# Group C's low-rank inputs projected with features as rows, their squares summed at reload, and four-head query jobs in a new order

## The chip, the cores and the metric

The kernel runs on one core of one Trainium2 chip. The time is the device time of one execution in microseconds, as the median of several runs. TensorE (PE) multiplies matrices and transposes, VectorE (DVE) and ScalarE (ACT) work elementwise, GpSimd (POOL) does a few products, and SyncE (SP) issues nearly all transfers between HBM and the on-chip memory. Matmul results go to PSUM, which has eight banks.

## The reference, cut to what matters

Two layers of a mixer. In each, one input projection feeds three groups of attention heads and a gate. 512 latent tokens and 256 context tokens go through the same weights; in the second layer context tokens need keys and values only.

```python
h = rms(x, norm_w[l]) * (1.0 + scale[:, None]) + shift[:, None]
u = h @ w_in
qa, ka, va, qb, kb, vb, cq, ckv, kpe, z = jnp.split(u, split_points(), axis=-1)
qa = rms(heads(qa, H_A), qn_a)                                  # group A, 8 heads of 64
qb = rms(heads(qb, H_B), qn_b)                                  # group B, 12 heads, 4 key/value heads
qc = rms(heads(rms(cq, qa_norm) @ w_qb, H_C), qn_c)             # cq: 768 low-rank features
kvc = heads(rms(ckv, kva_norm) @ w_kvb, H_C)                    # ckv: 512 low-rank features
...
x = x + gate[:, None] * merge_out(o_a, o_b, o_c, z, w_out[l])
```

Group C's queries, keys and values come from a second projection of cq and ckv. Their rms norms need, per token, the sum of squares over all 768 or 512 features. The norm's factor is a number per token, so it can be applied behind the second projection.

## The kernel before, in words

**Numbers as pairs.** Every float32 operand is split into a high and a low part, and each product is made of three matmuls: high x high, high x low, low x high. Weight pieces of 128x512 are loaded (`ws`), split by ScalarE (`wh`) and VectorE (`wl`), and used. The normalised input h lies on the chip as 16 pairs of tiles, 128 features x 768 tokens each; these 32 tiles come from the pool `s3`, which has 52 tiles in all. Heads' queries (one tile per head), keys (two), values (one), tables and probabilities come from the same pool.

**Two kinds of projection jobs.** `TJob` (line 429) puts tokens in rows: the stationary operand is a 128x128 block of h, the weights stream, 256 columns in most jobs; the results of two token tiles fill a PSUM bank. A job has eight steps of two k-blocks each. `FJob` (line 524) puts features in rows: a 128x128 weight block is stationary, and h streams, 384 tokens wide in two halves in layer 0 or 512 wide in layer 1; a job has four steps of four k-blocks and yields 128 features for all tokens. The gate z is made with FJobs (`zjob`, line 1487), and so is the shared rotary key (`kpe`, with the weights stacked).

**Chunks.** `kv_job` and `q_job` (lines 1529 and 1532) are TJobs of four 64-wide blocks. A key/value job has two key heads and two value heads. A query job has two heads of group A and two blocks of low-rank features (kind `"c"`), or three heads of group B and one such block; cq's 12 blocks ride along this way, and ckv's eight fill two jobs of four blocks (`GC`, "C"). Behind each job `post_chunk` (line 936) copies the banks out, squares them on ScalarE, sums the squares per block on VectorE, turns these into norms (`rsqrt`), applies the rotary tables for group B, transposes every pair of blocks on TensorE, and writes the heads' tiles. For blocks of kind `"c"` the sums go into `ssc`, and the transposed block is stored to HBM (`cscr`).

**Reload.** `prep_C` and `prep_one` (lines 1585 and 1608) load the low-rank features back, 128 at a time, four tiles of ckv and then six of cq, and split them into pairs with the gain applied. It takes three tiles of `s3` for each, and only when seven are free. `prep_norm` (line 1594) makes the norms `rq_eps` and `rkv` from `ssc`. `free_h` (line 926) gives the 32 tiles of h back when the last gate job is done. Then `q_jobs(0)` (line 1624) begins the second projection, followed by `w_kvb` jobs and group C's attention.

**What sets the order.** The kernel is recorded by a planner written in Python (`Weaver`, line 77). Strands of work run against an estimated clock of each engine, and each instruction is put on its engine's queue when the planner's turn comes; on the chip every queue runs in this order and waits on semaphores. The main strand runs the list of jobs one after the other; two worker strands run attention units in between, other strands load weights, split them and compute the modulation of the next layer (`ada_vec`, on VectorE). Where the free tiles do not suffice, a strand stands still: a job's last step waits until `room` (line 1109) finds tiles for its results plus two.

**The list of jobs** (layer 0; `layer`, line 1321, at its end): group A in four turns of one key/value job, one gate job, one query job of two heads, then attention of these two heads. The first turn's key/value and query jobs are cut in halves, with three gate jobs between. Group B in four turns: a key/value job in every other one, one or two gate jobs, a query job of three heads, attention. Then the two jobs of ckv, kpe, and the last gate jobs. Layer 1 has the same list with another first turn, and its query jobs cover four token tiles.

Of the kernel before, what the change touches and what calls it, by code (L numbers as in the profile page):

```python
# [18 lines left out]
OP = mybir.AluOpType  # L19
# [504 lines left out]
class FJob:  # L524


    def __init__(self, K, W, c0, segs, rhs, evs, post, stack=False, room=None):
        self.K, self.W, self.c0, self.segs = K, W, c0, segs
        self.rhs, self.evs, self.post, self.stack, self.room = rhs, evs, post, stack, room
        self.ps = [None] * len(segs)  # L530
        self.np = 4
        self.inS = False
        self.done = [Event() for _ in segs]
# [12 lines left out]
    def step(self, p):  # L546
# [32 lines left out]
        K.drop(hi, lo)  # L579

# [34 lines left out]
def body(K):  # L615
# [41 lines left out]
    ssc = K.st([128, 6, 20], name="ssc")  # L657
# [268 lines left out]
    def free_h():  # L926
        for k in range(KT):
            K.put("s3", hT[0][k], hT[1][k])
            hT[0][k] = hT[1][k] = None
        return None  # L930
# [5 lines left out]
    def post_chunk(G, grp, blocks, tiles, cscr, ev_c, rope, part=None):  # L936
# [9 lines left out]
        def gen(ps, done):  # L946
# [5 lines left out]
            for b, ts in enumerate(banks):  # L952
# [31 lines left out]
                if nn < ns:  # L984
                    c0 = blocks[nn][1]
                    nc.vector.tensor_copy(ssc[:, ts[0]:ts[0] + 2, c0:c0 + ns - nn],
                                          ss[:, b * 2 * ns:(b + 1) * 2 * ns].rearrange("p (t b) -> p t b", b=ns)[:, :, nn:])
                    w.bump("dve", 0.1)
# [26 lines left out]
            for bp in range(ns // 2):  # L1015
                pair = blocks[2 * bp:2 * bp + 2]
                pk = [b[0] for b in pair]
                for seg in ("lat", "ctx"):
# [6 lines left out]
                    for b in bs:  # L1025
                        for ti in range(len(banks[b])):
                            o = pt[:, i * 128:(i + 1) * 128]
                            if grp == "A" and seg == "lat" and pk[0] != "c":
                                o = pt.rearrange("p (b r c) -> p r b c", b=4 if pk[0] == "q" else 8, r=8)[:, 2 * i:2 * i + 2]
                            K.tr(o, raws[b][:, ti * 256 + bp * 128:ti * 256 + bp * 128 + 128])  # L1030
                            i += 1
# [3 lines left out]
                    if pk[0] != "c" and (rope is None or seg == "ctx"):  # L1035
                        j = (0 if grp == "A" else 2) + (pk[0] == "k")
                        gain = colA[:, j:j + 1]
                    if "c" in pk:
                        a = pk.index("c") * 64
                        st = yield from K.get("tm")  # L1040
                        yield from K.act(st[a:, :n], pt[a:, :n])
                        keep = w.cur.ft
                        i = blocks[2 * bp + a // 64][1]
                        yield from K.store(cscr[i * 64:i * 64 + 128 - a, c0:c0 + n], st[a:, :n], (128 - a) * n * 4)
                        for x in pk[a // 64:]:
                            K.set(ev_c[i, seg])
                            i += 1
                        K.put("tm", st)
                        w.cur.ft = keep
                    for j, (kind, hd) in enumerate(pair):  # L1050
                        if kind == "c":
                            continue
# [68 lines left out]
    def room_chunk(G, blocks):  # L1121
        d = []
        for kind, i in blocks:
            d += {"q": [(G.Q, i)], "k": [(G.KH, i), (G.KL, i)], "v": [(G.V, i)], "c": []}[kind]
# [196 lines left out]
    def layer(l):  # L1321
# [17 lines left out]
        def small():  # L1339
# [3 lines left out]
            for j in range(4):  # L1343
                K.side(rowB[:, j * 64:(j + 1) * 64], bc(t["qn_b" if j < 3 else "kn_b"][l], 64))
# [11 lines left out]
            yield from K.ts(rowB[:, :192], rowB[:, :192], 0.125, OP.mult)  # L1356
# [149 lines left out]
        def chunk(G, grp, blocks, tiles, cut=None):  # L1506

            runs = []
            for kind, i in blocks:
                c0 = COL["cq"] + 64 * i if kind == "c" else COL[START[kind][grp == "B"]] + 64 * i  # L1510
# [7 lines left out]
            def post(ps, done):  # L1518
# [4 lines left out]
                yield from post_chunk(G, grp, blocks, tiles, cscr, ev_c, rope, part)(ps, done)  # L1523
# [8 lines left out]
        def q_job(G, grp, heads, c, cut=None):  # L1532
            return chunk(G, grp, [("q", h) for h in heads] + [("c", i) for i in c], qt, cut)
# [3 lines left out]
        ev_c = {(i, s): Event() for i in range(20) for s in ("lat", "ctx") if s == "lat" or i >= 12 or not last}  # L1537
# [47 lines left out]
        def prep_C():  # L1585
            for key, nf, n, gain, b0 in (("kv", 4, TOK, kvaT, 12), ("q", 6, ntok, qaT, 0)):
                for f in range(nf):
# [3 lines left out]
                    w.spawn(prep_one(key, f, n, gain, b0 + 2 * f, raw, hi, lo), 2)  # L1591
                    yield None

        def prep_norm():
            yield from K.wait(*ev_c.values())
            tot = yield from sm()
            nt = len(qt)
            yield from K.red(tot[:, 0:nt], ssc[:, 0:nt, 0:12])
            yield from K.ts(tot[:, 0:nt], tot[:, 0:nt], 1.0 / 768, OP.mult, EPS, OP.add)
            yield from K.ts(rq_eps[:, 0:nt], tot[:, 0:nt], EPS, OP.mult)  # L1600
            yield from K.red(tot[:, 8:14], ssc[:, :, 12:20])
            yield from K.rsqrt(rkv, tot[:, 8:14], 1.0 / 512)
            K.put("sm", tot)
            K.set(ev_rkv)

        ev_rkv = Event()

        def prep_one(key, f, n, gain, b, raw, hi, lo):
            yield from K.wait(*(e for (i, _), e in ev_c.items() if i in (b, b + 1)))
            yield from K.load(raw[:, :n], cscr[b * 64:b * 64 + 128, :n], 512 * n)  # L1610
            yield from K.hilo(hi[:, :n], lo[:, :n], raw[:, :n], gain[:, f:f + 1])
            K.put("s3", raw)
            cT[key, f] = (hi, lo)
            K.set(ev_cT[key, f])
            K.put("ck", 0)

# [12 lines left out]
        def post_qC(p, rnd):  # L1629
            def gen(ps, done):  # L1630
                yield from K.wait(ev_kpe, ev_rkv)
# [316 lines left out]
        for p in range(4):  # L1948
            cut = HALF if not last and p == 0 else None
            kv = kv_job(GA, "A", 2 * p, cut)  # L1950
            q = q_job(GA, "A", (2 * p, 2 * p + 1), (2 * p, 2 * p + 1), cut)
            if cut:

                zs = [zjob(f) for f in (10, 11, 12)]
                q[0].inS = zs[2].inS = True
                jobs.extend([Group([kv[0], q[0]]), Group(zs), Group([kv[1], q[1]]), zjob(p)])
            elif last:
                z = zjob(p)
                jobs.extend([kv, z, q] if p else [Group([q, z]), kv])
            else:  # L1960
                jobs.extend([kv, zjob(p), q])
            J(lambda p=p: [attend64(GA, "A", h, h, h // 2) for h in (2 * p, 2 * p + 1)] and None)
            if p == 2:
                J(lambda: w.spawn(prep_B(), 1))
        zq = {0: [4, 5], 1: [6], 2: [7, 8], 3: [9]}
        for g in range(4):
            if g % 2 == 0:
                jobs.append(kv_job(GB, "B", g))
            for f in zq[g]:
                jobs.append(zjob(f))  # L1970
            jobs.append(q_job(GB, "B", range(3 * g, 3 * g + 3), (8 + g,)))
            J(lambda g=g: [attend64(GB, "B", h, g, 4 + h // 2) for h in range(3 * g, 3 * g + 3)] and None)
        for i in (12, 16):
            jobs.append(chunk(GC, "C", [("c", i + j) for j in range(4)], allt))
        jobs.append(FJob(K, W, COL["kpe"], [(0, 384), (384, 768)], rhs_h, ev_h, post_kpe, stack=True))
        J(lambda: (w.spawn(prep_C(), 3), w.spawn(prep_norm(), 2)) and None)
        for f in range(10 if last else 13, KT):
            jobs.append(zjob(f))
        J(free_h)
# [167 lines left out]
```

## Time and profile before

| what | value |
|---|---|
| median of 3 runs | 2937.42 us (2935.22 to 2939.45) |
| the profiled execution, whole | 2933.86 us |
| its span, first to last instruction | 2932.0 us |
| instructions | 54116 |
| busy: PE, PEld | 2808.8 us, 2645.5 us |
| busy: DVE, ACT, POOL | 2013.5 us, 1237.3 us, 148.5 us |
| mean granted TensorE clock | 0.989 of full speed |

PE is the matmuls, PEld the loads of the stationary operand, which overlap them. A row of the groups reads: line, engine, operation, output and inputs by tile name, shapes, count, then busy time and mean nanoseconds of one, then idle time of the engine ahead of it and what ended that. Nearly every matmul has line 333 and every transpose line 336, since helpers record them, so groups are told apart by tiles and shapes: `g<-wh,s` is a matmul of a TJob, `g<-s,wh` one of an FJob, `S<-s,s` are scores, `g<-pt,s` probabilities times values. A row of the timeline starts with the start time and the duration; a duration holds the pipeline's length, so the pace is read from start to start.

### The profile page before, as it was taken

What the parts mean: (1) busy time and instruction counts of PE and PEld (TensorE: products, weight loads), DVE (VectorE), ACT (ScalarE), POOL (GpSimd) and SP (SyncE); (2) the same over time, 40 slices, a digit from 0 to 9 for tenths busy, and PEclk for the clock granted to TensorE, in tenths of its full rate; (3) what the DMA queues carried; (4) which work ended last, traced back from release to release, by engine and by line L of the source; (5) the groups of instructions that cost most, each with busy time, mean ns of one, the idle gap of its engine ahead of it and who ended that gap; (6) DMA issues with size and microseconds to landing.
All of it is one profiled execution on the core that took longest, in us unless ns stands there. A gap on an engine that the chain in (4) does not pass through costs nothing.

```text
span 2932.0 us, 54116 instructions
## 1 busy us (share of the span) xinstructions
PE 2808.8 (96%) x20218; PEld 2645.5 (90%) x20218; DVE 2013.5 (69%) x5277; ACT 1237.3 (42%) x2692; POOL 148.5 (5%) x221
## 2 busy tenths in 40 slices
PE   5999999999999999989999999999999999999998
PEld 3779999999999999979998789999998999889987
DVE  6247776676887878989964385666667686488643
ACT  5223443342543554546421263434444455356421
POOL 3000100000111001000000000000000000000000
PEclk9999999999999999999999999999999999999999
DMA  9764433433323234323443453444342423412253
GB/s 263 248 193 122 115 107 112 116 95 111 90 81 98 85 109 148 121 75 128 144 135 118 126 156 103 116 116 117 92 116 67 114 84 103 137 45 85 90 176 118
DMA packets 408119, 350.09 MB, mean 119 GB/s; under 512 B 66532, under 2 KB 336914, under 8 KB 407856
## 3 DMA queue, kind: packets, MB, share of 16 engines
q1 hardware_dynamic: 405984, 345.32, 39.6%
q8 instruction: 159, 2.61, 0.4%
q0 software_dynamic: 1872, 1.32, 0.4%
q14 instruction: 104, 0.85, 0.1%
HBM read 305.01 MB, written 32.07 MB: 115 GB/s over the span
## 4 chain that ended last, share of the span: by engine, by line
PE 79%; DVE 11%; DMA 5%; SPq 2%; issue 2%; ACT 2%; DVEq 0%; ACTq 0%
PE g L333 63%; PE S L333 9%; PE g L336 5%; DMA s<-w_ada 2%; SPq L303 2%; DVE s L239 2%; DVE wl L239 2%; DVE s L272 2%; DMA s<-scr 1%; ACT s L233 1%; DVE pt L239 1%; DVE ac L261 1%; DVE s L261 1%; DVE tm L239 1%; PE g L799 1%
## 5 line engine op out<-in xcount | busy, mean ns | idle before, releaser
L333 PE MATMUL g<-wh,s 128*128 128x256 f32 (+2 forms) x7976 | 1641.9, 295 | 15.7 <-DVE s L239 4.7
L333 PEld LDWEIGHTS g<-wh,s 128*128 128x128 f32 x7976 | 1303.6, 192 | 43.1 <-issue 10.0
L333 PE MATMUL g<-wl,s 128*128 128x256 f32 (+2 forms) x3988 | 1167.6, 293 | 5.3 <-DVE wl L239 5.2
L333 PEld LDWEIGHTS g<-wl,s 128*128 128x128 f32 x3988 | 767.0, 192 | 20.0 <-DVE wl L239 11.0
L239 DVE TENSOR_TENSOR wl<-ws,wh 128x512 fp32r<-128x512 f32 (+1 forms) x606 | 413.3, 683 | 490.2 <-PE g L333 292.8
L233 ACT ACTIVATE wh<-ws 128x512 fp32r<-128x512 f32 (+2 forms) x614 | 377.5, 616 | 450.5 <-PE g L333 393.8
L333 PE MATMUL g<-s,wh 128*128 128x384 f32 (+1 forms) x1600 | 451.2, 357 | 1.1 <-DVE s L239 0.6
L233 ACT ACTIVATE s<-s,sm 128x512 f32<-128x512 f32 (+3 forms) x260 | 192.5, 740 | 392.9 <-DVE sm L272 323.3
L261 DVE SCALAR_TENSOR_TENSOR ac<-wa,scT,ac 128x512 f32<-128x512 f32 x420 | 312.4, 761 | 6.8 <-DMA wa<-w_ada 6.2
L333 PEld LDWEIGHTS g<-s,wh 128*128 128x128 f32 x1600 | 293.3, 188 | 24.7 <-issue 2.1
L333 PE MATMUL g<-s,wl 128*128 128x384 f32 (+1 forms) x736 | 261.5, 355 | 0.1
L333 PE MATMUL S<-s,s 128*128 128x256 f32 (+3 forms) x1260 | 235.5, 316 | 13.7 <-DVE sm L272 11.0
L336 PE MATMUL g<-ident,s 128*128 128x128 f32 x1488 | 226.8, 279 | 16.7 <-DVE s L256 8.2
L233 ACT ACTIVATE tm<-g 128x512 f32<-128x512 f32 (+3 forms) x298 | 146.5, 513 | 211.6 <-PE g L333 127.9
L333 PE MATMUL g<-pt,s 128*128 128x256 f32 (+1 forms) x1348 | 217.4, 290 | 16.1 <-DVE pt L239 12.2
L239 DVE TENSOR_TENSOR pt<-g,pt 128x512 fp32r<-128x512 f32 (+1 forms) x306 | 187.6, 623 | 55.6 <-ACT pt L233 54.1
L233 ACT ACTIVATE pt<-g 128x512 fp32r<-128x512 f32 (+1 forms) x306 | 159.8, 543 | 128.4 <-PE g L336 122.9
L333 PEld LDWEIGHTS S<-s,s 128*128 128x128 f32 x1260 | 187.3, 192 | 29.6 <-DVE sm L272 17.5
L333 PEld LDWEIGHTS g<-pt,s 128*128 128x128 f32 x1348 | 186.4, 195 | 24.1 <-DVE pt L239 17.2
L336 PEld LDWEIGHTS g<-ident,s 128*128 128x128 f32 x1488 | 174.7, 143 | 31.9 <-DVE s L256 11.2
L282 POOL TENSOR_TENSOR s<-ot,s 64x256 f32<-64x256 f32 x100 | 87.2, 873 | 1471.9 <-DVE ot L239 1383.8
L333 PEld LDWEIGHTS g<-s,wl 128*128 128x128 f32 x736 | 138.9, 189 | 10.0 <-DVE wl L239 0.8
(156 smaller groups left out, 2483.7 us busy)
## 6 DMA issues: line engine op xcount, KB each, us to landing
wa<-w_ada SPq DMA_DIRECT2D x256, 256.0 KB
ws<-w_in SPq DMA_DIRECT2D x328, 128.0 KB
ws<-w_in SPq DMA_DIRECT2D x160, 256.0 KB
ws<-w_out SPq DMA_DIRECT2D x144, 256.0 KB
s<-w_ada SPq DMA_DIRECT2D x128, 256.0 KB
s<-scr SPq DMA_DIRECT2D x36, 384.0 KB
ws<-w_in SPq DMA_DIRECT2D x64, 192.0 KB
ws<-w_qb SPq DMA_DIRECT2D x54, 192.0 KB
```

Source lines behind the costliest of these rows:

```text
L233: self.nc.scalar.activation(out, in_, func, bias=bias, scale=scale, **kw)
L239: self.nc.vector.tensor_tensor(out, a, b, op=op)
L261: self.nc.vector.scalar_tensor_tensor(out, a, s, b, op0=op0, op1=op1)
L272: self.nc.vector.tensor_tensor_reduce(out, a, b, -1.0, init, OP.add, OP.min, acc)
L282: self.nc.gpsimd.tensor_tensor(out, a, b, op=OP.mult)
L303: self.nc.sync.dma_start(out, in_)
L333: self.nc.tensor.matmul(out, l, r, start=start, stop=stop, skip_group_check=True)
L336: self.nc.tensor.transpose(out, in_, self.ident)
L799: nc.tensor.matmul(pt[:, 2 * c + m:2 * c + m + 1], a[:, c * 128:(c + 1) * 128], one, start=c == 0 and m == sides[0], stop=c == n // 128 - ...
```

## The change

- Low-rank features leave the chunks. Each 128 of them become an FJob (`cjob`): features as rows, ten jobs per layer (six for cq, four for ckv), whose post step copies the result out of PSUM and stores it to `cscr`. No transposes, no squares and no sums there.
- `prep_one` squares the reloaded tile in place on ScalarE, after its split, and VectorE adds it to the tile of its key's first feature block. After the last, `prep_norm` sums over the partitions with one one-column matmul per token tile, and makes `rq_eps` or `rkv` from it. `post_qC` waits for `ev_rq`, its own norm, and no longer for `rkv`.
- Query jobs have four heads: two for group A, three for group B.
- The jobs stand in a written list: low-rank jobs of ckv lie between those of groups A and B, and three of cq's lie right ahead of kpe.
- `free_h` frees eight tiles of h after each step of the last gate job.

The diff, cut to its core:

```diff
@@ FJob.step
         K.drop(hi, lo)
+        if self.after is not None:
+            self.after(p)
@@ body
-    def free_h():
-        for k in range(KT):
+    def free_h(p):
+        for k in range(4 * p, 4 * p + 4):
             K.put("s3", hT[0][k], hT[1][k])
@@ post_chunk
-                if nn < ns:
-                    c0 = blocks[nn][1]
-                    nc.vector.tensor_copy(ssc[:, ts[0]:ts[0] + 2, c0:c0 + ns - nn], ...)
...
-                    if "c" in pk:
-                        a = pk.index("c") * 64
-                        st = yield from K.get("tm")
-                        yield from K.act(st[a:, :n], pt[a:, :n])
-                        yield from K.store(cscr[i * 64:i * 64 + 128 - a, c0:c0 + n], st[a:, :n], (128 - a) * n * 4)
@@ layer
+        def cjob(f):
+            sg = segs if f < 6 or not last else [(0, 384), (384, 768)]
+            def post(ps, done):
+                for i, (a, b) in enumerate(sg):
+                    yield from K.wait(done[i])
+                    u = yield from K.get("tm")
+                    yield from K.act(u[:, :b - a], ps[i][:, :b - a])
+                    K.put("g", ps[i])
+                    yield from K.store(cscr[f * 128:(f + 1) * 128, a:b], u[:, :b - a], 512 * (b - a))
+                    K.put("tm", u)
+                K.set(ev_c[f])
+            return FJob(K, W, COL["cq"] + f * 128, sg, rhs_h, ev_h, post)
@@ prep_one
             yield from K.hilo(hi[:, :n], lo[:, :n], raw[:, :n], gain[:, f:f + 1])
-            K.put("s3", raw)
             cT[key, f] = (hi, lo)
             K.set(ev_cT[key, f])
             K.put("ck", 0)
+            yield from K.act(raw[:, :n], raw[:, :n], AF.Square)
+            if f == 0:
+                squares[key] = raw
+            else:
+                yield from K.wait(ev_sq[key, f - 1])
+                yield from K.add(squares[key][:, :n], squares[key][:, :n], raw[:, :n])
+                K.put("s3", raw)
+            K.set(ev_sq[key, f])
+            if f == nf - 1:
+                w.spawn(prep_norm(key, n // 128), 2, w.cur.ft)
@@ prep_norm
+            for ti in range(nt):
+                nc.tensor.matmul(ps[:, ti:ti + 1], q[:, ti * 128:(ti + 1) * 128], one, ...)
@@ post_qC
-                yield from K.wait(ev_kpe, ev_rkv)
+                yield from K.wait(ev_kpe, ev_rq)
@@ the list of jobs
+        jobs.extend([kv_job(GB, "B", 0), zjob(4), zjob(5), q_job(GB, "B", range(0, 4))])
+        jobs.extend([cjob(3), cjob(4), cjob(5)])
...
-        J(free_h)
+        jobs[-1].after = free_h
```

How the instructions stand afterwards is seen from the built programs. In both layers together TensorE has 2592 fewer matmuls of 256 columns, 1344 more of 384, 288 more of 512, 108 fewer transposes and 22 new one-column matmuls. VectorE has 27 fewer sums over 512 columns, 52 fewer copies into `ssc` and 16 more additions of whole tiles; ScalarE has 64 fewer copies or squares of 512 columns, 28 more copies of 384 and 20 more squares of 768 or 512. SyncE issues 128 fewer transfers of `w_in`, since four blocks side by side now load as one.

On TensorE, the end of layer 0's input projections: the last gate job's step, then the first job of group C's second projection (`s_14451` and `s_14452` are the pair of its first input).

```order
L333 MATMUL g<-s_2016,wh 128x384
L333 MATMUL g<-s_2016,wl 128x384
L333 MATMUL g<-s_2017,wh 128x384
L333 MATMUL g<-wh,s_14451 128x384
L333 MATMUL g<-wl,s_14451 128x384
L333 MATMUL g<-wh,s_14452 128x384
```

And VectorE there, in the changed kernel: `qaT` rows make the low parts of cq's inputs, `s_13482` is the tile in which the squares are summed, `wl` rows split weights.

```order
L261 SCALAR_TENSOR_TENSOR s_13594<-s_13592,qaT,s_13593 128x768
L239 TENSOR_TENSOR s_13482<-s_13482,s_13523 128x768
L239 TENSOR_TENSOR wl<-ws,wh 128x384
L261 SCALAR_TENSOR_TENSOR s_13599<-s_13597,qaT,s_13598 128x768
L239 TENSOR_TENSOR pt<-g,pt 128x512
L239 TENSOR_TENSOR s_13482<-s_13482,s_13592 128x768
```

The additions stand among the low parts and the weight splits; before, nothing of this kind lay there.

## The prediction on record

> **What bounds the kernel now.** First the page of the profile: busy shares, the slices of TensorE and VectorE, the chain by engine.
>
> ```profile
> span 2932.0 us, 54116 instructions
> PE 2808.8 (96%) x20218; PEld 2645.5 (90%) x20218; DVE 2013.5 (69%) x5277; ACT 1237.3 (42%) x2692; POOL 148.5 (5%) x221
> PE   5999999999999999989999999999999999999998
> DVE  6247776676887878989964385666667686488643
> PE 79%; DVE 11%; DMA 5%; SPq 2%; issue 2%; ACT 2%; DVEq 0%; ACTq 0%
> ```
>
> TensorE is busy in nearly every slice, and 79% of the chain that ended last is its own work. So a matmul that goes is worth its own pace, as long as nothing else comes late; VectorE, at 80% and more in twelve of the 40 slices, is what makes TensorE wait where it waits. The change lies in the input projections (about 200 to 1160 us in layer 0, 1740 to 2490 in layer 1) and at the point where group C's second projection takes over (1160 and 2490).
>
> A busy share doesn't say what one matmul costs, because matmuls overlap. The timeline of TensorE gives the pace, from start to start, for the three widths and for the two small kinds that the change touches:
>
> ```profile
> 474.36 0.40 PE L333 MATMUL g<-wh,s 128*128 128x256 f32 x2
> 474.60 0.28 PE L333 MATMUL g<-wl,s 128*128 128x256 f32 x1
> 474.72 0.40 PE L333 MATMUL g<-wh,s 128*128 128x256 f32 x2
> ...
> 1122.90 0.51 PE L333 MATMUL g<-s,wh 128*128 128x384 f32 x2
> 1123.25 0.33 PE L333 MATMUL g<-s,wl 128*128 128x384 f32 x1
> 1123.42 0.51 PE L333 MATMUL g<-s,wh 128*128 128x384 f32 x2
> ...
> 2511.57 0.62 PE L333 MATMUL g<-s,wh 128*128 128x512 f32 x2
> 2512.03 0.39 PE L333 MATMUL g<-s,wl 128*128 128x512 f32 x1
> 2512.26 0.62 PE L333 MATMUL g<-s,wh 128*128 128x512 f32 x2
> ...
> 1086.91 1.84 PE L799 MATMUL g<-one,ac 128*128 128x1 f32 x16
> 1088.62 1.64 PE L333 MATMUL g<-s,wh 128*128 128x384 f32 x8
> ```
>
> ```profile
> 1128.02 0.87 PE g L336 x8
> ```
>
> Three matmuls of 256 columns take 474.72 - 474.36 = 0.36 us, so 0.120 each; of 384 columns 0.52 us, 0.173 each; of 512 columns 0.69 us (0.68 between other pairs), 0.227 each. A matmul of one column takes 1.71 / 16 = 0.107, a 128x128 transpose 0.87 / 8 = 0.109 (the last row is the chain's).
>
> Where TensorE waits in the stretches that the change touches, the windows say:
>
> ```profile
> 785.00:800.00 15.00, 14.52 (x120) 14.21 (x120) 12.67 (x33) 9.29 (x21) 1.47 (x2) 1.00 0.33 104
> 800.00:820.00 20.00, 14.35 (x63) 11.62 (x64) 15.43 (x47) 9.72 (x27) 1.44 (x2) 0.67 0.21 60
> 1150.00:1160.00 10.00, 10.00 (x63) 9.97 (x62) 4.62 (x7) 3.38 (x6) 3.85 (x8) 1.00 0.63 198
> 1160.00:1200.00 40.00, 35.11 (x204) 32.96 (x204) 33.17 (x82) 20.67 (x44) 4.27 (x8) 0.91 0.62 191
> 2230.00:2270.00 40.00, 34.50 (x197) 30.19 (x197) 30.10 (x102) 19.74 (x54) 3.41 (x4) 0.87 0.22 61
> ```
>
> The columns are the stretch, its length, busy time (and count) of PE, PEld, DVE, ACT and POOL, the granted clock, the DMA share and GB/s. I price a wait as the idle time plus the busy time that a lower clock stretches: 800 to 820 loses 5.65 + 14.35 x 0.33 = 10.4 us, 1160 to 1200 loses 4.9 + 3.2 = 8.1, 2230 to 2270 loses 5.5 + 4.5 = 10.0.
>
> **Part by part: the matmuls.** A job of 256 weight columns with the tokens as rows takes 16 k-blocks x 3 products x 6 token tiles = 288 matmuls of 256 columns (192 with layer 1's four query tiles). Layer 0 has ten such jobs for queries and low-rank inputs, afterwards five: 1440 fewer. Layer 1 has 8 x 192 + 2 x 288 = 2112, afterwards 5 x 192 = 960: 1152 fewer. In their place come ten jobs of 128 features: in layer 0 each 16 x 3 x 2 = 96 of 384 columns (960), in layer 1 four such (384) and six of 48 with 512 columns (288). Removed: 2592 x 0.120 = 311.0 us. Added: 1344 x 0.173 + 288 x 0.227 = 232.5 + 65.4 = 297.9. Balance -13.1. The columns that stream are equal (2592 x 256 = 1344 x 384 + 288 x 512 = 663,552); the gain is that 960 fewer matmuls pay the constant of about 13 ns that the three paces have in common.
>
> The Trainium skill, page "TensorE: Matmul & The Clock Gate", section "Back-to-back issue gap", gives an isolated gap of N / 2.4 + 2.5 ns at the full clock, which speaks against this gain: as an estimate from that page the matmuls would bring 960 x 2.5 ns = 2.4 us, not 13. The trace does not agree: its 256-column matmuls stand 120 ns apart, not 109, so the sum keeps the rows.
>
> **Transposes and squares.** Two block pairs per job, a transpose per pair and tile: 12 per job of six tiles, 8 per job of four. Layer 0 falls from 120 to 60, layer 1 from 64 + 24 to 40: 108 x 0.109 = -11.8 us. The sums of squares now cross the partitions by a matmul with a column of ones: 22 x 0.107 = +2.4 us. TensorE's balance is -13.1 - 11.8 + 2.4 = -22.5 us. All of it lies in stretches where TensorE is busy, so I count it whole.
>
> **Vector and scalar engines.**
>
> ```profile
> L266 DVE TENSOR_REDUCE sm<-tm 128x8 f32<-128x512 f32 x52 | 35.5, 683 | 25.8 <-ACT tm L233 25.6
> L986 DVE COPY ssc<-sm x52: 169/170/543, 237.6 to 2466.4; 128x4 f32<-128x4 f32 x20, 128x2 f32<-128x2 f32 x20, 128x8 f32<-128x8 f32 x12
> L239 DVE TENSOR_TENSOR s<-s,s 128x768 fp32r<-128x768 f32 x16 | 15.3, 955 | 2.2 <-ACT s L233 2.2
> L239 DVE TENSOR_TENSOR s<-s,s 128x512 fp32r<-128x512 f32 x48 | 32.7, 688 | 7.0 <-ACT s L233 6.7 <-DMA s<-w_ada 0.3
> L233 ACT ACTIVATE s<-s 128x768 f32<-128x768 f32 x28 | 23.3, 840 | 45.1 <-DVE s L239 33.3 <-DMA s<-ctx 11.6
> ```
>
> VectorE loses 27 reductions (18.4 us) and 52 copies (8.8), and gains 16 additions, 11 x 0.955 + 5 x 0.688 = 13.9 us: 13 us less. ScalarE gains 20 squares at reload (0.84 us each at 768) and 28 copies of 384 columns, and loses 64 passes over 512 columns in the post steps. Neither is on the path by itself; the numbers matter for the waits. The 16 additions fall where group C takes over. The same rotary work in three jobs of four heads instead of four of three costs nothing: elements are equal, and a projection in front hides it. One weight piece now comes by one transfer instead of two, so SyncE issues fewer; nothing waited for it there, so I put it at 0.
>
> **The wait at 800 us.** This is the first group B key/value job in layer 0, the TensorE order of before: behind its next-to-last step stand 42 rows of attention alone, before the last step follows (the rows with wh and wl are the job's).
>
> ```order
> L333 MATMUL g<-wh,s_1897 128x256
> L333 MATMUL g<-wl,s_1897 128x256
> L333 MATMUL g<-wh,s_1898 128x256
> L336 MATMUL g<-ident,s_9675 128x128
> L336 MATMUL g<-ident,s_9710 128x128
> L336 MATMUL g<-ident,s_9675 128x128
> L336 MATMUL g<-ident,s_9710 128x128
> L336 MATMUL g<-ident,tm 128x128 x2
> ```
>
> The same place in the changed kernel, the same job's last two steps:
>
> ```order
> L333 MATMUL g<-wh,s_2010 128x256
> L333 MATMUL g<-wl,s_2010 128x256
> L333 MATMUL g<-wh,s_2011 128x256
> L1377 MATMUL g<-tm,flip 128x256
> L333 MATMUL g<-wh,s_2007 128x256
> L333 MATMUL g<-wl,s_2007 128x256
> L333 MATMUL g<-wh,s_2008 128x256
> ```
>
> The job no longer stands still for six free tiles: projections and attention alternate up to its end, and no stretch of attention alone as long as the old one is left between the projections. In the trace that stretch is one wait behind the other, each for VectorE:
>
> ```profile
> 802.26 0.74 PE L333 MATMUL S<-s,s 128*128 128x256 f32 x4 [1.01 <-DVE sm L272]
> 805.46 0.33 PE L336 MATMUL g<-ident,s 128*128 128x128 f32 x1 [1.85 <-DVE pt L239]
> 808.22 0.47 PE L333 MATMUL g<-pt,s 128*128 128x128 f32 x1 [1.68 <-DVE pt L239]
> ```
>
> With projections in between these would be covered. Of the 10.4 us I take 8, since VectorE's work (15.4 of 20 us busy) still has to be done nearby. Bounds: 0 and 10.4.
>
> **The handover at 1160 us.** Before, the tiles of h are freed after the last gate job, and the second projection of group C waits for the reload of its inputs:
>
> ```profile
> 1159.27 7.45 DMA s<-scr
> ...
> 1166.74 0.94 ACT s L233
> ```
>
> Now each of the last gate job's four steps frees eight tiles, so reloads start up to three steps earlier: 3 x 24 x 0.173 = 12.5 us. That covers the 7.45. What replaces it on TensorE's queue (rows around the ones; s_13524 and s_13593 are the third and fourth of the six inputs):
>
> ```order
> L333 MATMUL g<-wh,s_13524 128x384
> L333 MATMUL g<-wl,s_13524 128x384
> L333 MATMUL g<-wh,s_13525 128x384
> L1622 MATMUL g<-one,s_13482 128x1 x6
> L333 MATMUL g<-wh,s_13593 128x384
> L333 MATMUL g<-wl,s_13593 128x384
> ```
>
> The six one-column matmuls now stand ahead of the fourth input, and wait for the sum over all six; behind them three inputs' matmuls are queued, and the post step that frees PSUM waits for the norm. If the reloads come early, this costs nothing; if they come late, a square, an addition and 27 matmuls are delayed, 0.84 + 0.96 + 4.7 = 6.5 us. I take 1. Of the 8.1 us I take 5 (bounds 0 and 8.1).
>
> **Sum.** -22.5 - 8 - 5 + 1, and an allowance of +6 for new short waits: a new order makes some, and the one at 2230, as dear as 10 us, shows what one costs. Together -28.5 us. The profiled execution took 2933.9 us with a span of 2932.0, 3.6 under the median of 2937.4; the difference carried to the median gives 2909.
>
> **Rivals.**
> 1. The waits stay or move; only TensorE's work goes: -22.5 + 1, 2916 us. For it: VectorE's load falls by only 13 of 2013 us. Chance 0.22.
> 2. All three waits go, with no new one: -22.5 - 10.4 - 8.1 - 10.0, 2886 us. For it: VectorE has less to do in both layers. Chance 0.13.
> 3. Only columns count: the matmuls bring nothing, the transposes and ones -9.4, the waits -6: 2922 us. Against it: the three paces above. Chance 0.06. (The page's rule of the skill named above would come near this one; the trace disagrees with it.)
> 4. The squares delay the handover in both layers, and the old waits stay: -22.5 + 2 x 6.5, 2928 us, with the price open upwards. For it: VectorE is full right behind 1160. Against it: the reloads start 12.5 us earlier. Chance 0.07, counted as no change.
> 5. Slower: four heads' query tiles are taken at once, in a pool of 52 of which h holds 32; key/value jobs stand still at their last step for six tiles, as at 800 us. Four such holds in place of one: -22.5 + 1 + 3 x 10.4 = +9.7, 2947 us; it decides from the third new hold on. Against it: the rows of the order above, and low-rank jobs, which need no tile, stand between the others. Chance 0.06.
>
> **How the numbers follow.** The forecast has 0.46. Faster by over 0.2% (5.9 us, about what can be told from no change) holds for the forecast and rivals 1 to 3: 0.87; same 0.07; slower 0.06. The range from 2889 to 2928 leaves out about half of rival 2, half of rival 4 and rival 5, 0.16 together.
>
> **What would show it.** Right: 256-column matmuls down by 2592, paces unchanged, PE busy near 2786 us, no window of the input projections under 0.9 of the clock except small ones, and no DMA wait of 7 us in the chain at the handover. Wrong: a stretch of attention alone with a low clock in the projections, a wait of TensorE in front of the one-column matmul, or a span that falls by less than 15 us while the counts are as said.

## The result, and the profile after

The changed kernel takes 2906.02 us, the median of 4 runs (2901.62 to 2908.21), against 2936.53 us before, now the median of 4 runs. The ratio is 0.9893 with a 95% interval from 0.9876 to 0.9910: faster by 1.1%, 30.5 us. The forecast was 2909 us in a range from 2889 to 2928. The profiled execution took 2901.62 us, the fastest of the four, so its span understates the median by some 4 us.

The page of the changed kernel, first the same lines as before:

```profile
span 2899.8 us, 51534 instructions
PE 2775.4 (96%) x19194; PEld 2604.4 (90%) x19194; DVE 1995.0 (69%) x5099; ACT 1220.0 (42%) x2652; POOL 155.4 (5%) x217
PE   5999999999999999989989999999999999999998
DVE  5347676767897688989873385655657867598643
PE 79%; DVE 10%; DMA 5%; issue 2%; SPq 2%; ACT 2%; DVEq 0%; ACTq 0%
```

Nothing has changed in kind: TensorE is the bound in nearly every slice, and the chain is its work as before. There is just less of it.

TensorE's idle time, the span less its busy time, has not fallen: 2932.0 - 2808.8 = 123.2 us before, 2899.8 - 2775.4 = 124.4 after, and 123.3 in a second execution of the changed kernel (span 2907.7, busy 2784.4). What fell is busy time. Part of it is instructions that went, part is the granted clock, whose mean was 0.989 before and 0.995 and 0.992 after: a matmul at a lower clock counts as busy for longer (three of 384 columns take 0.96 us from 1154.48 on in the first run of experiment 1, at a clock of 0.66 from 1145 to 1160, instead of 0.52). As an estimate, busy time times mean clock goes from 2777.9 to 2761.5 and 2762.1, so about 16 us are TensorE's work, to some 3 us since the clocks are rounded. The two executions of the changed kernel differ by 7.9 us with nearly the same idle time.

The groups of TensorE by form show the trade, and the new squares:

```profile
L333 PE MATMUL g<-wh,s 128*128 128x256 f32 x5440 | 1050.7, 287 | 12.9 <-DVE tm L239 6.4 <-DVE pt L239 1.8 <-ACT s L233 1.8
L333 PE MATMUL g<-wl,s 128*128 128x256 f32 x2720 | 771.4, 284 | 0.0
L333 PE MATMUL g<-s,wh 128*128 128x384 f32 x1984 | 529.6, 339 | 1.1 <-DVE s L239 0.6 <-ACT s L233 0.4
L333 PE MATMUL g<-s,wh 128*128 128x512 f32 x704 | 232.9, 396 | 0.0
L1622 PE MATMUL g<-one,s 128*128 128x1 f32 x44 | 5.2, 245 | 0.0
```

256-column matmuls of the weight's high and low part are down to 8160, 2592 fewer, as counted. The last row has 44 instructions where the program has 22: a float32 matmul of this kind is recorded as two.

The windows that answer to those of before (columns as there):

```profile
690.00:740.00 50.00, 49.62 (x316) 48.89 (x315) 41.13 (x107) 25.37 (x63) 2.87 (x4) 1.00 0.35 106
825.00:850.00 25.00, 22.29 (x167) 21.57 (x166) 23.13 (x70) 15.28 (x43) 1.44 (x2) 1.00 0.24 67
1140.00:1180.00 40.00, 35.48 (x224) 34.01 (x223) 32.50 (x85) 18.73 (x43) 8.90 (x15) 0.96 0.55 142
2200.00:2250.00 50.00, 50.00 (x422) 50.00 (x421) 36.19 (x102) 20.17 (x48) 6.30 (x6) 1.00 0.33 95
```

In the input projections no stretch is left with a clock of 0.67 or 0.87; the worst is the one from 825 to 850, 2.7 us idle at full clock. Layer 1's wait at 2230 is gone too. At the handover, 1140 to 1180, 4.5 us of idle are left. The timeline there names what TensorE waits for now:

```profile
1141.95 0.34 PE L333 MATMUL g<-wh,s 128*128 128x384 f32 x1
...
1147.13 0.44 PE L333 MATMUL g<-wl,s 128*128 128x384 f32 x1 [1.72 <-DVE wl L239]
...
1148.66 1.50 PE L1622 MATMUL g<-one,s 128*128 128x1 f32 x12
1150.02 0.42 PE L333 MATMUL g<-wh,s 128*128 128x384 f32 x1
...
1160.75 0.44 PE L333 MATMUL g<-wh,s 128*128 128x384 f32 x1 [2.64 <-ACT wh L233]
```

The first row is the first matmul of group C's second projection. The reload is not waited for any more: the chain's 7.45 us on it are gone. What TensorE waits for instead are this projection's own weights, once their low part on VectorE and once their high part on ScalarE, and behind that a transfer, which the chain names:

```profile
1152.38 7.68 DMA ws<-w_qb
1160.13 0.04 issue
1160.17 0.53 ACT wh L233
1160.73 0.57 DVE wl L239
```

The one-column matmuls, six of them in twelve instructions, take 1.36 us from start to start and wait for nothing. But the wait of 1.72 us for `wl` has to do with the squares. VectorE is busy from 1136 us on, and the additions of squares (`s<-s,s`) stand in its queue ahead of that `wl`; the last one ends as the one-column matmuls begin:

```profile
1141.35 0.95 DVE L239 TENSOR_TENSOR s<-s,s 128x768 f32<-128x768 f32 x1
...
1143.15 0.95 DVE L239 TENSOR_TENSOR s<-s,s 128x768 f32<-128x768 f32 x1
...
1145.99 1.08 DVE L239 TENSOR_TENSOR wl<-ws,wh 128x384 fp32r<-128x384 f32 x1
...
1147.66 0.95 DVE L239 TENSOR_TENSOR s<-s,s 128x768 f32<-128x768 f32 x1
```

**Where the time went, by two marks.** The start of group C's second projection is easy to find in each trace, as the first 384-column matmul of its first query job in each layer. Before it stands at 1161.4 us in layer 0 and 2543.8 in layer 1, with the end at 2932.0; afterwards at 1141.9, 2515.2 and 2899.8. So 19.4 us are won up to the first mark, 9.1 between the marks, 3.7 behind the second. The second execution of the changed kernel has 1145.3, 2522.7 and 2907.7, which makes 16.1, 5.0 and 3.2: a mark of one execution is good to a few us only. (In layer 1 the prediction put the takeover at 2490; by the trace it is at 2543.8.)

The waits at the handover itself lie behind the first mark, since the projection's first inputs are there when it begins. They are seen in its first two query jobs, of 54 matmuls each. The first takes 17.0 us before and 12.9 in both executions of the changed kernel; the second takes 11.1 before, 14.1 and 14.6 after. Together they take 28.1 us before, 27.0 and 27.5 after.

### The profile page after: what moved, and what is told of

Read it like the earlier page. It is cut to its first block, busy times and chain, and to the rows that moved or that the text cites. A ratio compares the mean times of both kernels' runs of the same rounds, so it can differ in the third digit from the quotient of the medians.

```text
span 2899.8 us, 51534 instructions
## 1 busy us (share of the span) xinstructions
PE 2775.4 (96%) x19194; PEld 2604.4 (90%) x19194; DVE 1995.0 (69%) x5099; ACT 1220.0 (42%) x2652; POOL 155.4 (5%) x217
## 4 chain that ended last, share of the span: by engine, by line
PE 79%; DVE 10%; DMA 5%; issue 2%; SPq 2%; ACT 2%; DVEq 0%; ACTq 0%
PE g L333 62%; PE S L333 9%; PE g L336 5%; SPq L303 2%; DVE s L239 2%; DVE wl L239 2%; DVE s L272 1%; DMA s<-w_ada 1%; DVE ac L261 1%; DVE s L261 1%; ACT s L233 1%; DMA s<-scr 1%; DVE s L256 1%; PE g L801 1%; DVE tm L239 1%
## 5 line engine op out<-in xcount | busy, mean ns | idle before, releaser
L333 PE MATMUL g<-wh,s 128*128 128x256 f32 (+2 forms) x6248 | 1306.4, 298 | 18.1 <-DVE tm L239 6.4
L333 PEld LDWEIGHTS g<-wh,s 128*128 128x128 f32 x6248 | 1024.4, 192 | 46.5 <-ACT s L233 6.6
L333 PE MATMUL g<-wl,s 128*128 128x256 f32 (+2 forms) x3124 | 921.6, 295 | 5.4 <-DVE wl L239 5.0
L333 PE MATMUL g<-s,wh 128*128 128x384 f32 (+1 forms) x2688 | 762.5, 354 | 1.1 <-DVE s L239 0.6
L333 PEld LDWEIGHTS g<-wl,s 128*128 128x128 f32 x3124 | 599.9, 192 | 20.0 <-DVE wl L239 10.8
L333 PEld LDWEIGHTS g<-s,wh 128*128 128x128 f32 x2688 | 492.2, 188 | 31.5 <-issue 2.1
L333 PE MATMUL g<-s,wl 128*128 128x384 f32 (+1 forms) x1280 | 448.3, 350 | 0.3 <-DVE wl L239 0.3
L333 PEld LDWEIGHTS g<-s,wl 128*128 128x128 f32 x1280 | 240.9, 188 | 12.4 <-DVE wl L239 0.6
L336 PE MATMUL g<-ident,s 128*128 128x128 f32 x1488 | 223.6, 277 | 12.9 <-DVE s L239 5.7
L333 PE MATMUL g<-pt,s 128*128 128x256 f32 (+1 forms) x1348 | 210.0, 285 | 8.7 <-DVE pt L239 6.2
L233 ACT ACTIVATE tm<-g 128x512 f32<-128x512 f32 (+2 forms) x238 | 113.3, 494 | 212.9 <-PE g L333 134.2
```

Of the source, the lines that this page charges most:

```text
L233: self.nc.scalar.activation(out, in_, func, bias=bias, scale=scale, **kw)
L333: self.nc.tensor.matmul(out, l, r, start=start, stop=stop, skip_group_check=True)
L336: self.nc.tensor.transpose(out, in_, self.ident)
```

## The experiments

Twelve runs were made, ten edits (one of them measured twice) and the changed kernel once more, each timed against the kernel before. The first mark is that of layer 0, the second that of layer 1. "Handover" is the time from the first mark to the last matmul of the two query jobs, "idle" is the span less TensorE's busy time. Marks, handover, idle and span are of the profiled execution.

| kernel | median, us | ratio to before, 95% interval | first mark | handover | second mark | idle | span |
|---|---|---|---|---|---|---|---|
| before, as first measured | 2936.5 | 1 | 1161.4 | 28.1 | 2543.8 | 123.2 | 2932.0 |
| changed, as first measured | 2906.0 | 0.9893 (0.9876 to 0.9910) | 1141.9 | 27.0 | 2515.2 | 124.4 | 2899.8 |
| changed, again | 2903.8 | 0.9895 (0.9880 to 0.9910) | 1145.3 | 27.5 | 2522.7 | 123.3 | 2907.7 |
| changed, h freed late | 2897.1 | 0.9864 (0.9851 to 0.9877) | 1144.1 | 37.4 | 2512.9 | 113.4 | 2897.5 |
| the same, again | 2893.7 | 0.9859 (0.9845 to 0.9874) | 1142.6 | 37.0 | 2509.8 | 110.7 | 2894.3 |
| before, h freed early | 2930.0 | 0.9976 (0.9966 to 0.9987) | 1164.6 | 26.0 | 2536.4 | 122.4 | 2924.1 |
| old form, new list, h freed early | 2924.6 | 0.9963 (0.9951 to 0.9974) | 1156.8 | 25.6 | 2539.0 | 121.7 | 2922.5 |
| old form, new list, h freed late | 2926.5 | 0.9972 (0.9961 to 0.9984) | 1158.8 | 29.3 | 2539.1 | 122.8 | 2922.3 |
| changed, low-rank jobs last | 2949.5 | 1.0052 (1.0038 to 1.0065) | 1173.8 | 22.6 | 2554.5 | 139.0 | 2944.3 |
| changed, 256 tokens wide | 2893.1 | 0.9853 (0.9839 to 0.9868) | 1150.6 | 27.3 | 2505.7 | 104.8 | 2890.6 |
| the same, h freed late | 2900.6 | 0.9878 (0.9863 to 0.9893) | 1148.4 | 29.2 | 2515.5 | 110.8 | 2900.1 |
| changed, no squares | 2891.4 | 0.9854 (0.9837 to 0.9870) | 1141.2 | 23.7 | 2502.4 | 114.1 | 2886.6 |
| changed, pace 5.0 | 2897.0 | 0.9868 (0.9855 to 0.9882) | 1142.7 | 26.9 | 2512.7 | 116.1 | 2895.9 |
| changed, 256 wide, pace 5.0 | 2902.0 | 0.9892 (0.9875 to 0.9908) | 1149.7 | 27.5 | 2514.0 | 109.9 | 2897.3 |

My theory was: 20 us of the gain is TensorE's own work, 10 are waits that the list and the early freeing took away. The rivals were that only streamed columns cost time, that the order is worth nothing, and that the early freeing carries the waits.

**1. h freed late in the changed kernel.**

```diff
-        jobs[-1].after = free_h
+        J(lambda: [free_h(p) for p in range(4)] and None)
```

> The changed kernel (2906 us) with all 32 tiles of h freed at the end of the last gate job, as before. My theory (about 20 us of the gain is TensorE's own work, about 10 us are waits that went, one of them the reload at the handover to group C) expects the reload's wait back in layer 0: 2911 us, between 2908 and 2914. The rival that the reload was hidden anyway expects 2906, and the rival that the early freeing carries all of the waits' 10 us expects 2916.

Measured 2897.1: 9 us less, where I expected 5 more. The wait for the reload does come back. The chain of this kernel at the handover:

```profile
1140.98 5.00 DMA s<-scr
1146.01 0.94 ACT s L233
...
1148.49 13.34 DMA ws<-w_qb
1161.91 0.53 ACT wh L233
```

The handover takes 37.4 us instead of 27.0 and 27.5, so the late freeing costs 10 us there, twice what I had expected. The first mark (1144.1) can't show this wait, since it lies behind it. But by the last matmul of group C's query jobs the loss is made up (1328.9 us, against 1324.7 and 1328.4), and by the second mark more than that. So the wait that the early freeing removes is real, and removing it wins nothing here in the end. It was measured again beside the changed kernel on one chip:

> The changed kernel with h freed at the end, measured once more, now beside the changed kernel on one chip. The first time it came out at 2897, 9 us under the changed kernel, where I had expected 5 over it. If that was the order that the late freeing gives behind the handover (VectorE's work in group C's first attention less crowded), it stays 4 to 9 us under the changed kernel; if it was the chip, the two agree within 3 us; my first theory still says 2 to 8 over.

> The changed kernel unchanged, on one chip with the next three, so that they can be compared with it directly. Expected 2903 to 2908 us, as first measured.

2893.7 against 2903.8. The intervals of the ratios (0.9845 to 0.9874, and 0.9880 to 0.9910) do not overlap: the difference of 10 us is not the chip. The handover takes 37.0 us here, and TensorE idles 113.4 and 110.7 us in the two executions, against 124.4 and 123.3.

**2. Only the early freeing, in the kernel before.** The diff is the part of the change on `FJob.step`, `free_h` and `jobs[-1].after`.

> The kernel before (2936.5 us) with only the early freeing of h added. My theory expects 5 us less, 2931 (2928 to 2934), with the wait of 7.45 us for the reload gone from the chain. If the early freeing carries all of the waits' gain, 2926; if it is worth nothing by itself, 2936.

Measured 2930.0, 5.4 us less than before (2935.4 here): the size that I expected. But most of it comes from another place. The chain at the handover has the weights in the reload's place:

```profile
1167.98 0.41 SPq L303
1168.51 8.31 DMA ws<-w_qb
1176.93 0.53 ACT wh L233
```

The handover takes 26.0 us instead of 28.1, so 2 of the 5 us are won where I had put them. The first mark stands 3 us later than before, and the rest of the gain comes behind the handover, before the second mark. So a number that agreed did not show the mechanism.

**3. The old form in the new list.** Five jobs of four blocks with tokens as rows take the place of the ten low-rank jobs, at their places in the list; transposes, squares and sums are back behind the job.

```diff
-        jobs.extend([cjob(8), cjob(9), cjob(0), zjob(6), q_job(GB, "B", range(4, 8))])
+        jobs.extend([cC(16), zjob(6), q_job(GB, "B", range(4, 8))])
...
-        jobs.extend([cjob(3), cjob(4), cjob(5)])
+        jobs.append(cC(8))
```

> The new list of jobs with four-head query jobs and the early freeing, but the low-rank features projected in the old form: five jobs of 256 columns with tokens as rows, transposed, squared and summed behind the job. This separates form from order. My theory expects the TensorE work back, 13.1 + 11.8 - 4.5 = 20.4 us over the changed kernel, and the waits still gone: 2926 us (2922 to 2930). If only streamed columns cost time on TensorE, the matmuls cost nothing more and 7 us come back: 2913. If the gain is all in the form, none in the order, 2936.

Measured 2924.6. The form is worth 2906.0 - 2924.6 = -18.6 us against the first measurement of the changed kernel (-20.8 against the second): near the 20.4 us of TensorE's work, and not the 7 of the rival that only columns count. But the waits are not all gone, though I had expected that. From 813 to 832 us attention stands alone again, as at 800 us before the change:

```profile
800.00:850.00 50.00, 43.88 (x293) 41.09 (x292) 41.32 (x120) 25.29 (x69) 6.01 (x7) 0.86 0.23 69
```

By the prediction's way of pricing that is 6.12 + 43.88 x 0.14 = 12.3 us. So the difference holds this wait besides TensorE's work and can't tell the two apart; that it comes so near to 20.4 is partly luck. List, four-head query jobs and early freeing together are worth 10.8 us against the kernel before.

**4. The same with h freed late.** Edit as in 1.

> The new list of jobs with four-head query jobs, the low-rank features in the old form, and h freed at the end. With the early freeing this came to 2925. If the early freeing costs 10 us with the new list whatever the form, as it does in the changed kernel, 2915; if it brings what it brought to the kernel before (5 us), 2930; if it does nothing by itself, 2925. Against the changed kernel with h freed at the end (2894 to 2897) the form then has its own price once more: my theory expects 19 us, so 2914.

Measured 2926.5, 2 us over the early freeing. The early freeing brings 5 us before the change, 2 here (the two intervals overlap), and costs 7 to 10 with the new form: it has no price of its own. Between the two late kernels the form is worth 2926.5 - 2895.4 (the mean of the two measurements in 1) = 31 us, more than the 20 between the early ones.

**5. The low-rank jobs last.**

```diff
-        jobs.extend([cjob(3), cjob(4), cjob(5)])
+        jobs.extend([cjob(f) for f in (6, 7, 8, 9, 0, 1, 2, 3, 4, 5)])
```

All `cjob`s in front of it are gone from the list, and in group A's later turns the gate and query jobs stand in the old sequence.

> The changed kernel with the ten low-rank jobs of each layer put together right ahead of the shared rotary key, and the other jobs in the old turn order. TensorE's work is the same. My theory (projections between attention units cover VectorE's latencies, and a job that waits for tiles leaves attention alone) expects stands like the one at 800 us, about 10 us each, since stretches of attention alone appear once per layer: 2926 us (2916 to 2936). The rival that the order is worth nothing expects 2906.

Measured 2949.5: 43 to 46 us more than the changed kernel, and slower than before the change. The stretches of attention alone are back, one in each layer: from 690 to 723 us and from 2146 to 2179 us no matmul of a projection runs. The windows around them:

```profile
675.00:725.00 50.00, 38.57 (x238) 34.41 (x237) 40.52 (x121) 22.80 (x62) 5.46 (x6) 0.80 0.21 66
2150.00:2200.00 50.00, 40.69 (x256) 37.49 (x255) 38.09 (x121) 23.36 (x60) 6.87 (x8) 0.84 0.14 41
```

Idle time plus the stretching of a lower clock, as in the prediction: 11.4 + 38.57 x 0.20 = 19.1 us, and 9.3 + 40.69 x 0.16 = 15.8 us. These two come to 35 of the 43 to 46. Over the whole kernel TensorE idles 139.0 us instead of 124.4 and 123.3, at a mean granted clock of 0.984 instead of 0.995 and 0.992. So it is shown that such stretches cost this, nearly twice what I had put on one, and that this order brings them. That a job which waits for tiles leaves them is read from the order, and was not tested by itself.

**6. Stretches of 256 tokens.** The same columns in as many matmuls more as the change had saved, 960.

```diff
-            sg = segs if f < 6 or not last else [(0, 384), (384, 768)]
+            sg = [(a, a + 256) for a in range(0, SEQ if f < 6 and last else TOK, 256)]
```

> The changed kernel with its low-rank jobs in stretches of 256 tokens instead of 384 or 512: the same columns, but 960 matmuls more, as many as the change saved. My theory of a constant of about 13 ns for each matmul expects +12.8 us over the changed kernel, 2919 (2914 to 2924). If only columns cost, 2906; with a constant of 2.5 ns, which the Trainium skill gives in the page on TensorE and the clock gate, section on the back-to-back issue gap, as an estimate 2908.

Measured 2893.1: 10 us less, where the paces say 12.8 more. Up to the first mark they hold: 480 of the matmuls lie there, 6.4 us by the paces, and the mark stands at 1150.6 against 1141.9 and 1145.3, 5 to 9 us later. The pace itself is in the trace too, 0.120 us for each of these matmuls:

```profile
1030.06 0.40 PE L333 MATMUL g<-s,wh 128*128 128x256 f32 x2
1030.30 0.28 PE L333 MATMUL g<-s,wl 128*128 128x256 f32 x1
1030.42 0.40 PE L333 MATMUL g<-s,wh 128*128 128x256 f32 x2
```

What is lost there is won between the marks (1355 us against 1373 and 1377), and by waiting less: TensorE idles 104.8 us, the least of all. With h freed late:

> The changed kernel with both edits that had come out faster than it: low-rank jobs in stretches of 256 tokens, and h freed at the end. TensorE has 960 matmuls more than the changed kernel, +12.8 us by the paces; each edit alone came to about 2894 because fewer waits were left. If the two gains added up, 2884; if both only land on another order with its own waits, as I now think, anywhere from 2890 to 2910, with the input projections of layer 0 6 us longer than in the changed kernel with h freed at the end.

The first mark is 4 to 6 us later than in the kernels of experiment 1, again as the paces say, and the end comes at 2900.6, 7 us later than with the early freeing. Two edits that each won 10 us together win 3 to 5.

**7. No squares.** `prep_one` gives its tile back after the split, and the norms are set by a `memset`.

> The changed kernel without the squares, their additions and the one-column matmuls; the two norms of the low-rank inputs are set to one, so this part of the computation is left out. My theory expects the one-column matmuls' 4.5 us (22 of them, recorded as two instructions each, 12 of which took 1.23 us) and about 1 us at the handover: 2900 us (2897 to 2904). The rival that the squares hold up the handover in both layers expects 2893 or less.

Measured 2891.4, 12.4 us less than the changed kernel beside it. That is what the rival asked for, but the traces put most of it elsewhere. The first query job of the handover takes 9.4 us instead of 12.9. Of these 3.5 us, 1.4 are the six one-column matmuls, and about 2 are the wait for `wl` behind the additions on VectorE, which is gone. In layer 1, 536.6 us pass from the last 256-column matmul of the input projections to the end, instead of 539.8 and 540.1, and ten one-column matmuls make about 2 of that. So the squares cost some 2 us at the first handover and 1 around the second, not 6.5 at each as rival 4 has it. The largest part, 5 us against one execution of the changed kernel and 9 against the other, is won from layer 0's last query matmul to that point in layer 1, where no square lies. Other edits win as much there with the squares in, and where this part comes from stays open.

**8. A modulation step every 5.0 us.** Most of what the edits 1, 6 and 7 won, they won behind the handover of layer 0. One wait there could be the cause. The chain of the changed kernel, measured again, in the middle of layer 0's output projection:

```profile
1496.03 1.42 DVE ac L261 x2
...
1497.46 3.58 DMA wa<-w_ada
...
1501.14 1.43 DVE ac L261 x2
...
1502.58 4.10 DMA wa<-w_ada
...
1508.82 0.06 DVE tm L239
```

The `ac` rows accumulate the next layer's modulation, each from its piece of `w_ada`; the `tm` rows, which empty the PSUM banks of the output projection, stand behind them in VectorE's queue. I took the 3.58 and 4.10 us for time in which VectorE stands still. The planner lays these steps by a pace:

```diff
-PACE = [5.5, 2.0, 10.0]
+PACE = [5.0, 2.0, 10.0]
```

> The changed kernel with one number of the planner changed: a modulation step every 5.0 us instead of 5.5 during layer 0. In the changed kernel's chain VectorE stands 3.58 and 4.10 us in front of modulation steps whose weights have not landed, in the middle of layer 0's output projection, and TensorE behind it. My theory (waits come and go with the order that the planner happens to record; this is one of them) expects the modulation to be through earlier, and 3 to 10 us less than the changed kernel's 2904: 2897. The rival that this wait is covered anyway expects 2904, and that VectorE, fuller in the input projections, makes TensorE wait there, 2910.

Measured 2897.0, 7 us less than the 2903.8 of the changed kernel. The chain at this place has no such wait any more:

```profile
1490.00 1.56 PE g L801 x14
1491.56 8.63 PE g L333 x71
1500.27 0.06 DVE wl L239
...
1502.53 5.66 DMA tm<-ctx
```

But my reading of the chain was wrong. The 3.58 and 4.10 us are the times of the transfers, and VectorE ran other rows during them. In the changed kernel it idled 0.80 and 0.72 us ahead of these steps:

```profile
1501.14 2.74 DVE L261 SCALAR_TENSOR_TENSOR ac<-wa,scT,ac 128x512 f32<-128x512 f32 x4 [0.80 <-DMA wa<-w_ada]
1506.71 0.75 DVE L261 SCALAR_TENSOR_TENSOR ac<-wa,scT,ac 128x512 f32<-128x512 f32 x1 [0.72 <-DMA wa<-w_ada]
```

Nor are such waits new or dear. From 1440 to 1720 us VectorE waits 7.3 us for `w_ada` in this kernel, 6.2 in the kernel before, 3.7 with the new pace, and 12.3 with h freed late, which is 10 us faster. From layer 0's last query matmul to the first `S<-wh,s` of the output projection 228.8 us pass with the new pace, against 231.2 and 232.4: 2 to 4 of the 7 us at most. So the number fell into the range that I had given, and the reason is not shown. With 256 tokens the pace does the opposite:

> The changed kernel with stretches of 256 tokens (2893 by itself) and the modulation's pace of 5.0 us (2897 by itself). If the two gains were each tied to one wait and added up, 2886; if every edit only lands on another recorded order, 2890 to 2905. Either way it is the last try for a version faster than the changed kernel.

2902.0, 9 us over the same kernel at the old pace.

## Why the prediction was right, and where not

**TensorE's work: right.** Forecast -22.5 us, of which matmuls -13.1, transposes -11.8, one-column matmuls +2.4. The counts came as worked out, and PE's busy time at 2775.4 and 2784.4 us, where I had named 2786. The third term was mis-sized: I had read 16 rows as 16 matmuls, and they were eight, two instructions each, so one takes 0.205 us and the 22 take 4.5. That makes -20.4. TensorE's busy time at full clock fell by about 16 us by the estimate above, so -20.4 is if anything too much; experiment 3's -18.6 to -20.8 holds a wait as well. The constant of about 13 ns per matmul is seen in its place in experiment 6, as 0.120 us from start to start and as 5 to 9 us up to the first mark. As an estimate, the 2.5 ns that the Trainium skill's page "TensorE: Matmul & The Clock Gate", section "Back-to-back issue gap", gives for isolated matmuls would have made that 1.2 us (480 x 2.5 ns). The measurement speaks against it here.

**The wait at 800 us: right.** It is gone, and experiment 5 brings its like back, dearer. But neither the list nor the form removes it alone: the old form in the new list has it (experiment 3, where the first mark stands at 1157, only 5 us before the old one), and so has the new form in nearly the old order (experiment 5). Why the new form is needed, no run separates.

**The handover: wrong.** I took 5 of 8.1 us because the reloads start earlier. They do, and the wait for them goes: the first query job is 4.1 us shorter. But the second is 3.0 to 3.5 us longer, because the weights of the same projection then hold TensorE, and of the 5 us 0.6 to 1.1 are left (2.0 to 2.5 without the six one-column matmuls). The step that failed is to count the wait's removal as kept, with nothing of that size late behind it. With h freed late the handover costs 10 us more, and still the kernel is 7 to 10 us faster.

**The squares at the handover: near.** Taken at 1 us. TensorE doesn't wait for them, but VectorE's additions delay a `wl`, which costs about 2 us (experiment 7). Why leaving them out won 12.4 us in all stays open.

**The allowance of +6, and the waits as a whole: not shown.** No new wait was traced to a cause with its price. The sum took -8 - 5 + 1 + 6 = -6 us for waits. TensorE's idle time didn't fall at all (123.2 us before, 124.4 and 123.3 after), so other waits took the place of those that went; what fell besides TensorE's work is the time lost to a lower clock, in which layer 1's wait at 2230, on which I had counted nothing, has its part. So the total of -28.5 against -30.5 is closer than its parts, and that is luck.

**The rivals.** The rival that the order only moves waits has more truth than its 0.22: edits of little consequence to the work (experiments 1, 6 and 8) made this kernel 7 to 11 us faster than its second measurement, and on top of the 256-token edit two of them made it 7 to 9 us slower. None of these was slower than the changed kernel itself. The slower one, stands of attention for lack of tiles, is what experiment 5 made: 2949.5 us, near the 2947 that it was priced at; but that price was for four stands in another list, and here two dearer ones make most of it, so the agreement is chance.

The fastest versions are the changed kernel with 256 tokens (2893.1) and with h freed late (2893.7 and 2897.1), 7 to 13 us under it. Their TensorE idles 104.8, 110.7 and 113.4 us instead of 123 to 124, so they are faster by waiting less; why these orders wait less, I could not show.

## What to carry to other kernels

Where one engine is busy 96% of the time, count its instructions and price them by start-to-start paces; here the counts came out as said and the paces held. Putting the old form into the new order is a test of such a term only if no wait comes back with it; here one did. Don't price a single wait as if its removal were kept: look for what is late next on the same queue, and check the gain from a mark ahead of the wait to one right behind it, since a total that agrees can come from elsewhere. The time of a transfer in the chain is not idle time of the engine that follows it: read that from the engine's own rows. In a kernel whose order a planner records, the order itself moves the time by more than the noise (7 to 11 us here, where an interval reaches about 4 us to either side), so a change worth less than that needs more than one order to be judged by.

## What the runs showed of the hardware that was not expected

A float32 matmul of one column is recorded as two instructions and takes 0.205 to 0.227 us (six took 1.23 us in the chain at 1107 us and 1.36 from start to start at 1148.66), not the 0.107 us of one row. Before the change TensorE's granted clock was 0.67 from 800 to 820 us, where it idled 5.65 us and no single wait was longer than 1.85 us; the lost time there is nearly double the idle time. But short waits alone don't decide it: from 1220 to 1250 us in the changed kernel TensorE idled 8.4 of 30 us, no wait longer than 1.66 us, at a clock of 0.94. The pace of matmuls with float32r operands was 0.120, 0.173 and 0.227 us at 256, 384 and 512 columns: 53 to 54 ns for each 128 columns, and a constant of about 13 ns on top.
